# Neighbourhood attention scores in blocks of 32 queries on 64x32 tiles of TensorE

## The chip, the cores and the metric

The kernel runs on one core of a Trainium2 chip. The metric is the device time of one execution in microseconds; the median of three runs before the change is 994.35 us (994.02 to 994.75). The core has five engines with queues of their own: TensorE (PE in the profile; its weight loads are listed apart, as PEld), VectorE (DVE), ScalarE (ACT), GpSimd (POOL) and SyncE (SP), which issues almost all DMAs. Matrix products land in PSUM, which this kernel divides into eight banks of 128 partitions by 512 fp32 values.

## What is computed

One layer over 2048 tokens, laid out as 32 rows by 64 columns, with 16 heads of 64. A query attends to 8 rows by 16 columns around it, with a learned bias for each offset. Cut to what matters:

```python
def neighbourhood_attention(q, k, v, rpb):      # grid of 32 rows x 64 columns
    rs = clip(r - 4, 0, 32 - 8)                  # first key row of query row r
    q_cstart = clip(q_col - 8, 0, 64 - 16)       # first key column of a query column
    s = q . k * 64 ** -0.5 + rpb[head, key_row - r + 7, key_col - q_col + 15]
    s = where(key in the 8 x 16 window, s, -1e30)
    return softmax(s) . v

x = x + (neighbourhood_attention(q, k, v, rpb) * silu(gate)) @ w_out     # q, k, v, gate = rmsnorm(x) @ w_in
out = rmsnorm(x)
```

All matrices are fp32 and the output is compared as fp32.

## The kernel before

**Stages.** Two stages at the start form most of the input projection (groups pp and pv in the profile), then the attention runs, interleaved with the rest of the projection (pp, lines 392 to 396) and later with plain tiles of the output projection (po, lines 1580 to 1584), and a last stage forms the rest of the output projection (py, line 1674). In the profiled execution the attention runs from about 562 to 872 us.

**Cycles.** The attention has 32 cycles. A cycle belongs to a pair of heads p (0 to 7; s in the code is the head within the pair, on partitions 0 to 63 or 64 to 127) and a band T of 8 query rows (0 to 3). `order` (line 1220) runs first all pairs at T=0, then each pair at T=1 and T=2, then all pairs at T=3. A band needs the key rows of `KEY_ROWS`: 11, 15, 15 or 12 rows. The 64 columns are eight strips of 8; the 64 queries of a band and strip g form one block, and its keys lie in the strips g-1 to g+1.

**The order on the engines** is the order in which the program is written; nothing reorders it but semaphores. A cycle m of the main loop (line 1806) issues:

1. `begin(m)`: puts loads for later on a list with due times in units of matmuls (queries, keys, values, bias tables, gate); `due` issues them on SP's queue as the matmuls of `feed` go by.
2. `feed`: matmuls of the projection or of the output. A group of the projection accumulates 24 matmuls in one bank (`group`, line 383); `feed` stops after a given number of them, not at the end of a group. A cycle has some 13.5 of them in the dense part.
3. `normalise(2m-1)`: the second half of the last cycle's probabilities are divided by their sums (POOL, ACT, DVE).
4. `turns(m-1)`: the last cycle's probabilities are transposed on TensorE, 44 transposes of 64 queries by up to 120 keys (line 1357), into six banks (6, 8 and 8 blocks of 64 columns for each half of the partitions). ACT copies three of the banks to SBUF (line 1347), DVE the other three (line 1345).
5. `scores(2m)` and `scores(2m+1)`: each does two of the four `GROUPS` of strips. A group puts two strips on partitions 0 to 63 and 64 to 127 of a bank, so four matmuls of 64 queries (two strips, two heads) run on the four 64x64 quadrants of TensorE (line 1297). The strips 0 and 7 have two strips of keys (`WIDE` 2), the others three. All 64 queries of the band see all key rows of the band: 2 or 3 strips by 8 by 11, 15 or 12 columns. `score_places` (line 1276) gives a bank to each group and head, but puts the first two groups of a head in one bank where 5R fits 512 columns (R is key rows times 8: T=0 and T=3). DVE adds the bias table and finds the extreme (line 1306: the reduction that the page calls CUSTOM_DVE_ANT_0, followed by a read of its accumulator), writing to SBUF and thereby ending the use of the bank; ACT forms the exponential and its sum (line 1312).
6. `values(m-1)`: 16 matmuls of the transposed probabilities with the values into one bank (o, line 1376), on two halves of the columns side by side. DVE multiplies by the gate (line 1380); the result is stored through DRAM (line 1383).

**Buffers.** `banks` has eight buffers; the order of release sets which one is handed out next. `xp` has eight tiles for the scores (line 1303), which are taken anew in each cycle; `mp` has ten tiles for bias tables, of which a cycle at T=0, T=1 or T=3 loads three (`load_bias`, line 1261; T=2 uses those of T=1); `kp` has two tiles for keys (`load_k`, line 1228). In PSUM, a float32 matmul of the program makes two records in the trace; a transpose makes one.

Of the kernel before, what the change touches and what calls it, by code (L numbers as in the profile page):

```python
# [40 lines left out]
BIAS = [(u1 - u0) * 80 for u0, u1 in TYPE_ROWS]  # L41
# [3 lines left out]
def bias_tables(rpb):  # L45
    out = []
    for t, (u0, u1) in enumerate(TYPE_ROWS):
        T = (0, 1, 3)[t]
        got = []
        for G in (1, 0):  # L50
            qr, col, strip, kr, c = np.ogrid[T * 8:T * 8 + 8, :8, :WIDE[G], T * 8 + u0:T * 8 + u1, :8]
            half = []
            for g in GROUPS[G]:
                qc = g * 8 + col
                kc = (FIRST[g] + strip) * 8 + c
# [4 lines left out]
                half.append(np.where(ok, b, np.float32(NEG)).reshape(NP, 2, 64, -1))  # L60
            got.append(np.concatenate(half, axis=2).transpose(0, 2, 1, 3).reshape(NP, 128, -1))
        out += got
    return np.concatenate(out, axis=2)


def linear():
    at, n = {}, 0
    for strips in [(0,), (1, 2), (3, 4), (5, 6), (7,)]:
        for s in range(2):
            for strip in strips:  # L70
                for g in range(max(strip - 1, 0), min(strip + 2, 8)):
                    at[s, strip, g] = n
                    n += 1
    return at
# [3 lines left out]
def build(ctx, tc, x, xr, xt, wg, bias, w_out, n0, nf, out):  # L78
# [540 lines left out]
    def stage_one():  # L619
# [6 lines left out]
        land["x12"] = [rbp([128, 512], F32, "land") for _ in range(2)] + [kp([128, 960], F32, "land")[:, :512] for _ in range(2)]  # L626
# [30 lines left out]
        def value_rows(j):  # L657
            spot = mkp([128, 3, 512], F32, "vs")
            homes = [spot[:, k] for k in range(3)] + [kp([128, 960], F32, "vs")[:, :512]]
# [49 lines left out]
        def step(i):  # L709
# [3 lines left out]
            if i >= 2 * E:  # L713
                seven.after(n, P, then)
            elif P == 1:
                seven.keep(n, kp([128, 960], F32, "p1")[:, :512] if n > 3 else accs[n - 2] if n > 1 else None)
# [205 lines left out]
        def load_u1():  # L922
            for t in range(4):
                U1[t] = accs[t] if t < 2 else ep([128, 512], F32, "u1") if t == 2 else kp([128, 960], F32, "u1")[:, :512]
                nc.sync.dma_start(U1[t], vu1[t])
# [87 lines left out]
    def stage_two():  # L1013
# [11 lines left out]
        def out_rows(k):  # L1025
            def g():
# [5 lines left out]
                homes += [kp([128, 960], F32, "ow")[:, :512] for _ in range(4 - len(homes))]  # L1032
# [61 lines left out]
        def values_product(P, i):  # L1094
# [6 lines left out]
            if P == 1:  # L1101
                U1[i] = ep([128, 512], F32, "u1") if i < 2 else kp([128, 960], F32, "u1")[:, :512]
# [118 lines left out]
    pairs = [(p, T, (h, h + 1)) for p, T in order for h in (0, 2)]  # L1221
    N = len(pairs)
# [5 lines left out]
    def load_k(p, T):  # L1228
# [4 lines left out]
        def keys():  # L1233
            t = kp([128, 960], F32, "kt")
            KT[p, T] = t.rearrange("p (r c) -> p r c", c=GW)
            nc.sync.dma_start(t[:, :n], kd[p][:, r0 * GW:r1 * GW])
# [24 lines left out]
    def load_bias(p, ty):  # L1261
        n = (TYPE_ROWS[ty][1] - TYPE_ROWS[ty][0]) * 8
        a = sum(BIAS[:ty])
        fs = []
        for w in (3 * n, 3 * n, 4 * n):
            t = mp([128, 512], F32, "em")[:, :w]
            EM.setdefault((p, ty), []).append(t)
            fs.append(lambda t=t, a=a, w=w: nc.sync.dma_start(t, bias[p, :, a:a + w]))
            a += w
        i0, i1, e = EM[p, ty]  # L1270
        EM[p, ty] = [[e[:, :2 * n], e[:, 2 * n:]], [i0, i1]]
# [3 lines left out]

    def score_places(cs, R):
        at = {"order": [(C, s) for C in cs for s in range(2)]}
        if cs[0] == 0 and 5 * R <= 512:
            for s in range(2):
                b = bank(5 * R, f"s{s}")  # L1280
                at[0, s], at[1, s] = b[:, :2 * R], b[:, 2 * R:]
        else:
            for C, s in at["order"]:
                at[C, s] = bank(R * WIDE[C], f"s{s}")
        return at

    def scores(i, between=None):
        p, T, cs = pairs[i]
        kt, qt = KT[p, T], QT[p, T]
        r0, r1 = KEY_ROWS[T]  # L1290
        R = (r1 - r0) * 8
        places = score_places(cs, R)
        for C, s in places["order"]:
            for h, g in enumerate(GROUPS[C]):
                c0 = 8 * FIRST[g]
                a = slice(s * 64, s * 64 + 64)
                nc.tensor.matmul(places[C, s][h * 64:h * 64 + 64], qt[a, g * 64:g * 64 + 64],  # L1297
                                 kt[a, :r1 - r0, c0:c0 + 8 * WIDE[C]].rearrange("p r (s c) -> p s r c", c=8),
                                 start=True, stop=True, skip_group_check=True)
        got = [(C, [places[C, s] for s in range(2)]) for C in cs]  # L1300
        ST[i] = st = tiny.tile([128, 12], F32, name="st")
        for j, (C, pst) in enumerate(got):
            X[i, C] = [xp([128, 512], F32, f"x{s}")[:, :R * WIDE[C]] for s in range(2)]
            for s in range(2):
                o = 2 * j + s
                nc.vector.tensor_tensor_reduce(X[i, C][s], pst[s], EM[p, ROW_TYPE[T]][C > 0][s], -1.0, 1e38,  # L1306
                                               OP.add, OP.min, st[:, o:o + 1])
            if between and j == 0:
                between()
            for s in range(2):  # L1310
                o = 2 * j + s
                nc.scalar.activation(X[i, C][s], X[i, C][s], AF.Exp, bias=st[:, o:o + 1], scale=-1.0,  # L1312
                                     accum_out=st[:, 4 + o:5 + o])

    def normalise(i, both=False, between=None):
        st = ST.pop(i)
        nc.vector.reciprocal(st[:, 8:12], st[:, 4:8])  # L1317
        for j, C in enumerate(pairs[i][2]):
            for s in range(2):
                o = 8 + 2 * j + s  # L1320
                if both and j:
                    nc.vector.tensor_scalar(X[i, C][s], X[i, C][s], st[:, o:o + 1], None, op0=OP.mult)
                elif both and s:
                    nc.scalar.activation(X[i, C][s], X[i, C][s], AF.Copy, scale=st[:, o:o + 1])
                else:
                    nc.gpsimd.tensor_scalar(X[i, C][s], X[i, C][s], st[:, o:o + 1], 1.0, op0=OP.mult, op1=OP.mult)  # L1326
        if between:
            between()

    spots = linear()  # L1330

    def turns(m):
# [3 lines left out]
        t = PT[m].rearrange("p (n h c) -> p h n c", h=2, c=64)  # L1336
        ends = (6, 14, 22)
        size = (6, 8, 8)
        ph = {(b, h): bank(size[b] * 64, f"ph{h}") for b in range(3) for h in range(2)}
        left = {(b, h): size[b] for b in range(3) for h in range(2)}  # L1340

        def copy(b, h):
            o, i_ = t[:k, h, ends[b] - size[b]:ends[b]], ph[b, h][:k].rearrange("p (n c) -> p n c", c=64)
            if h:
                nc.vector.tensor_copy(o, i_)  # L1345
            else:
                nc.scalar.activation(o, i_, AF.Copy)  # L1347

        group = {g: C for C in range(4) for g in GROUPS[C]}
        home = lambda n: sum(n // 2 >= e for e in ends)  # L1350
# [545 lines left out]
```

## Time and profile before

| | before |
|---|---|
| median of three runs | 994.35 us (994.02 to 994.75) |
| span of the profiled execution | 993.1 us |
| TensorE busy | 985.0 us, 99% of the span |
| DVE, ACT, POOL busy | 774.3, 542.2, 127.3 us |
| scores on TensorE (line 1297) | 1024 records, 70.8 us busy |
| transposes (line 1357) | 1408 records, 47.0 us busy |
| values (line 1376) | 1024 records, 83.5 us busy |
| bytes moved by DMA | 227.65 MB, mean 229 GB/s |
| granted TensorE clock | 1.00 in all stretches but the last hundred microseconds (0.98) |

The span is measured by the profiler from the first to the last instruction of one execution; the runs are timed apart from it, and their median lies 1.25 us above this span. A row of the groups has the line, the engine, the operation, what it writes and reads, partitions by columns, the count, then the busy time in us and the mean duration in ns of one, then the idle time of the engine before them. Rows of the chain and of a timeline have the start in us, the length in us, and how many instructions are merged in the row; a timeline adds in brackets the idle time before and what ended it. Matmuls overlap, so their durations are longer than their spacing.

### The profile page before, as it was taken

The page shows a single profiled execution, that of the slowest core. Times are in us where ns is not written, and L with a number is a line of the kernel's source. Part 1 is how long each engine was busy: PE and PEld are TensorE (multiplying, and loading weights), DVE is VectorE, ACT ScalarE, POOL GpSimd, SP SyncE. Part 2 cuts the span into 40 slices and gives each one's busy share as a digit, 9 for nine tenths or more (in the row PEclk, how much of TensorE's full clock was granted, in tenths as well). Part 3 has the DMA queues.
Part 4 walks back from the last instruction along what each step waited for, and adds up shares of the span by engine and source line. Part 5 has one row for each costly group of instructions (what it writes and reads, how often), then busy time and mean ns, then how long its engine had stood idle before and what let it go on. Part 6 is the DMA issues. An engine that isn't in the chain of part 4 may idle for free.

```text
span 993.1 us, 19498 instructions
## 1 busy us (share of the span) xinstructions
PE 985.0 (99%) x6892; PEld 789.6 (80%) x6892; DVE 774.3 (78%) x1703; ACT 542.2 (55%) x1310; POOL 127.3 (13%) x204
## 2 busy tenths in 40 slices
PE   9999999999999999999999999999999999999997
PEld 7888888888888888888888777777677777788886
DVE  6899888987565876766775687778889888886866
ACT  7873245455535342343433377778778886663443
POOL 0000001231100000000000022223232321211110
PEclk9999999999999999999999999999999999999999
DMA  8943547777957836557455798978989888996754
GB/s 291 338 128 98 194 135 257 244 240 242 374 157 226 277 117 201 192 174 229 170 179 199 231 290 271 270 237 264 302 247 296 263 249 249 330 382 160 197 153 116
DMA packets 150121, 227.65 MB, mean 229 GB/s; under 512 B 13641, under 2 KB 65097, under 8 KB 150025
## 3 DMA queue, kind: packets, MB, share of 16 engines
q1 hardware_dynamic: 147000, 221.30, 69.5%
q0 software_dynamic: 2592, 4.72, 2.9%
q8 instruction: 54, 0.88, 0.3%
q10 hardware_dynamic: 432, 0.40, 0.1%
q14 instruction: 43, 0.34, 0.1%
HBM read 160.31 MB, written 66.06 MB: 228 GB/s over the span
## 4 chain that ended last, share of the span: by engine, by line
PE 97%; DMA 1%; ACT 1%; DVE 0%; issue 0%; SPq 0%; DVEq 0%
PE pp L448 40%; PE pv L614 13%; PE py L1674 12%; PE o L1376 8%; PE s L1297 6%; PE ph L1357 4%; PE pv L729 2%; PE pp L394 2%; PE pp L392 2%; PE pp L396 2%; PE po L1584 2%; PE po L1582 2%; PE po L1580 2%; DMA kt<-kd 1%; DMA vt<-vd 1%; ACT x L1312 0%
## 5 line engine op out<-in xcount | busy, mean ns | idle before, releaser
L448 PE MATMUL pp<-h,f 128*128 128x512 f32 x576 | 185.5, 390 | 0.0
L448 PE MATMUL pp<-t,f 128*128 128x512 f32 x702 | 171.5, 390 | 0.0
L448 PEld LDWEIGHTS pp<-t,f 128*128 128x128 f32 x702 | 131.7, 188 | 27.6 <-DVE u L461 0.3
L1326 POOL TENSOR_SCALAR x<-x,st 128x360 f32<-128x360 f32 (+5 forms) x160 | 81.5, 524 | 524.0 <-DVE st L1317 524.0
L1312 ACT ACTIVATE x<-x,st 128x360 f32<-128x360 f32 (+5 forms) x256 | 134.1, 525 | 24.7 <-DVE st L1306 24.6
L448 PEld LDWEIGHTS pp<-h,f 128*128 128x128 f32 x576 | 108.1, 188 | 22.7 <-ACT p L456 0.3
L448 PE MATMUL pp<-l,f 128*128 128x512 f32 x288 | 112.2, 389 | 0.0
L1306 DVE CUSTOM_DVE_ANT_0 x<-s,em 128x360 f32<-128x360 f32 (+5 forms) x256 | 102.7, 457 | 3.1 <-issue 1.6
L431 DVE TENSOR_TENSOR f<-raw,f 128x512 fp32r<-128x512 f32 x105 | 75.8, 727 | 19.9 <-ACT f L430 19.8
L1376 PEld LDWEIGHTS o<-pta,vt 120*64 120x64 f32 (+2 forms) x1024 | 68.8, 137 | 22.3 <-DVE st L1306 15.2
L430 ACT ACTIVATE f<-raw 128x512 fp32r<-128x512 f32 x105 | 63.5, 622 | 37.9 <-DVE raw L437 20.1
L1376 PE MATMUL o<-pta,vt 120*64 120x192 f32 (+5 forms) x1024 | 83.5, 316 | 0.0
L1297 PE MATMUL s<-kt,q 64*64 64x360 f32 (+5 forms) x1024 | 70.8, 412 | 0.9 <-DMA kt<-kd 0.9
L1347 ACT ACTIVATE pta<-ph 120x512 f32<-120x512 f32 (+5 forms) x96 | 49.2, 557 | 36.0 <-PE ph L1357 35.9
L1345 DVE COPY pta<-ph 120x512 f32<-120x512 f32 (+5 forms) x96 | 56.1, 638 | 13.3 <-PE ph L1357 13.0
L448 PEld LDWEIGHTS pp<-l,f 128*128 128x128 f32 x288 | 54.1, 188 | 11.3
L1674 PE MATMUL py<-woh,f 128*128 128x512 f32 x192 | 60.8, 390 | 0.0
L614 PE MATMUL pv<-wh,t 128*128 128x512 f32 x176 | 56.2, 389 | 0.0
L448 PE MATMUL pp<-sixths,f 128*128 128x512 f32 x198 | 52.7, 389 | 0.0
L1297 PEld LDWEIGHTS s<-kt,q 64*64 64x64 f32 x1024 | 36.2, 132 | 20.2 <-DVE pta L1345 1.0
L1357 PEld LDWEIGHTS ph<-ident,x 64*120 64x120 f32 (+2 forms) x1408 | 42.5, 128 | 11.3 <-issue 10.9
L430 ACT ACTIVATE f<-s 128x512 fp32r<-128x512 f32 x42 | 26.2, 624 | 45.9 <-DVE s L437 42.6
(227 smaller groups left out, 1875.9 us busy)
## 6 DMA issues: line engine op xcount, KB each, us to landing
raw<-in_wg_dram SPq DMA_DIRECT2D x124, 256.0 KB, 5.2
row<-in_xr_dram SPq DMA_DIRECT2D x32, 256.0 KB, 5.3
vd<-v SPq DMA_DIRECT2D x32, 256.0 KB, 4.9
sgd<-sg SPq DMA_DIRECT2D x32, 256.0 KB, 3.2
q<-qd SPq DMA_DIRECT2D x32, 256.0 KB, 6.8
sgt<-sgd SPq DMA_DIRECT2D x32, 256.0 KB, 7.0
ogd<-og SPq DMA_DIRECT2D x32, 256.0 KB, 3.4
kt<-kd SPq DMA_DIRECT2D x16, 480.0 KB, 6.9
```

The source lines that it names most:

```text
L430: nc.scalar.activation(t[:, 0], src, AF.Copy)
L431: nc.vector.tensor_tensor(t[:, 1], src, t[:, 0].bitcast(F32), OP.subtract)
L448: nc.tensor.matmul(B[n, P], t[:, int(m == 2), c], x[k][int(m == 1)], start=P in (1, 6, 5) and k == 0 and m == 0, stop=k == 3 and m == 2, s ...
L614: nc.tensor.matmul(p, a[:, o], b, start=P in (1, 6, 5) and k == 0 and m == 0, stop=k == 3 and m == 2, skip_group_check=True)
L1297: nc.tensor.matmul(places[C, s][h * 64:h * 64 + 64], qt[a, g * 64:g * 64 + 64], kt[a, :r1 - r0, c0:c0 + 8 * WIDE[C]].rearrange("p r (s c) ...
L1306: nc.vector.tensor_tensor_reduce(X[i, C][s], pst[s], EM[p, ROW_TYPE[T]][C > 0][s], -1.0, 1e38, OP.add, OP.min, st[:, o:o + 1])
L1312: nc.scalar.activation(X[i, C][s], X[i, C][s], AF.Exp, bias=st[:, o:o + 1], scale=-1.0, accum_out=st[:, 4 + o:5 + o])
L1326: nc.gpsimd.tensor_scalar(X[i, C][s], X[i, C][s], st[:, o:o + 1], 1.0, op0=OP.mult, op1=OP.mult)
L1345: nc.vector.tensor_copy(o, i_)
L1357: nc.tensor.transpose(ph[b, h][:k, o:o + 64], X[2 * m + late_, group[g]][s][q, at:at + k], ident[q, q])
L1376: nc.tensor.matmul(o[s * 64:s * 64 + 64, g0 * 64:g1 * 64], vt[:k, strip, s * 64:s * 64 + 64], t[:k, n * 64:(n + g1 - g0) * 64], start=stri ...
L1674: nc.tensor.matmul(B[m, P], t[:, a, c], b, start=P in (1, 6, 5) and k == 0 and i == 0, stop=k == 3 and i == 2, skip_group_check=True)
```

## The change

The 64 queries of a band and strip are split into two halves of 4 rows by 8 columns. A matmul of scores now has 32 queries as its stationary side and runs on a tile of 64x32: two heads by four strips (`quad` 0: strips 0 to 3, 1: strips 4 to 7) fill TensorE's eight such tiles at once. Each half sees its own 11 key rows (8 at the grid's upper and lower edge; `HALF_ROWS`) by 24 columns, for all strips alike. So that strips 0 and 7 can be 24 columns wide too, the tile of keys gets 8 more columns at each end, which hold the neighbouring row's keys or zeros; the bias tables have -1e30 there.

- A cycle's scores are 32 matmuls instead of 16; each half and head has a bank of its own, four for each of the two calls, at every T.
- The tiles of scores are taken once (`make_x`) and hold 3 strips by 120 keys; what a half does not see is set to zero there once (and again by `clear_x` after the last cycle at T=0). Reductions, exponentials and divisions work on three blocks of 88 or 64 columns.
- The transposes are 48 instead of 44, in three rounds of 16, each into two banks of 512 columns that are allocated in that round.
- The values' matmuls read the transposed probabilities in blocks of 32 columns.
- The bias tables come by the kind of half (`top`, `mid`, `end`) and `quad`: four loads for a cycle at T=0 and T=3, two for T=1 and T=2 together. The tiles of `mp` grow from 512 to 528 columns, those of `kp` from 960 to 1024.

The diff, cut to its core:

```diff
-ROW_TYPE = [0, 1, 1, 2]
-TYPE_ROWS = [(0, 11), (-4, 11), (-4, 8)]
-GROUPS = [(0, 7), (2, 1), (4, 3), (6, 5)]
-FIRST = [0, 0, 1, 2, 3, 4, 5, 6]
-WIDE = [2, 3, 3, 3]
+HALF_ROWS = [[(0, 8), (0, 11)], [(0, 11), (4, 11)], [(0, 11), (4, 11)], [(0, 11), (4, 8)]]
+TABLES = {"mid": (8, 4, 11), "top": (0, 0, 8), "end": (28, 24, 8)}
+TABLE_AT = {"mid": 0, "top": 1056, "end": 1824}
...
-    pairs = [(p, T, (h, h + 1)) for p, T in order for h in (0, 2)]
+    pairs = [(p, T, quad) for p, T in order for quad in range(2)]
...
-            t = kp([128, 960], F32, "kt")
-            KT[p, T] = t.rearrange("p (r c) -> p r c", c=GW)
-            nc.sync.dma_start(t[:, :n], kd[p][:, r0 * GW:r1 * GW])
+            KT[p, T] = t = kp([128, 1024], F32, "kt")
+            lo, hi = 8 * (r0 > 0), 8 * (r1 < ROWS)
+            if not lo:
+                nc.gpsimd.memset(t[:, :8], 0.0)
+            if not hi:
+                nc.gpsimd.memset(t[:, 8 + n:16 + n], 0.0)
+            nc.sync.dma_start(t[:, 8 - lo:8 + n + hi], kd[p][:, r0 * GW - lo:r1 * GW + hi])
...
+    kinds_of = lambda T: {0: ("top", "mid"), 3: ("mid", "end")}.get(T, ("mid", "mid"))
+
+    def load_bias(p, T):
         fs = []
+        for kind in dict.fromkeys(kinds_of(T)):
+            w = 48 * TABLES[kind][2]
+            for quad in range(2):
+                t = mp([128, 528], F32, "em")[:, :w]
+                for half in range(2):
+                    if kinds_of(T)[half] == kind:
+                        EM[p, T, quad, half] = [t[:, :w // 2], t[:, w // 2:]]
+                o = TABLE_AT[kind] + quad * w
+                fs.append(lambda t=t, o=o, w=w: nc.sync.dma_start(t, bias[p, :, o:o + w]))
...
+    def keys_of(t, half, T):
+        u, n = HALF_ROWS[T][half]
+        return t.rearrange("p (s k) -> p s k", s=3)[:, :, 8 * u:8 * u + 8 * n]
...
     def scores(i, between=None):
+        p, T, quad = pairs[i]
         kt, qt = KT[p, T], QT[p, T]
+        places = {}
+        for half, (u, n) in enumerate(HALF_ROWS[T]):
+            for s in range(2):
+                places[half, s] = bank(24 * n, f"s{s}")
+            for h in range(4):
+                g = 4 * quad + h
+                for s in range(2):
+                    a = slice(s * 64, s * 64 + 64)
+                    o = u * GW + 8 * g
+                    nc.tensor.matmul(places[half, s][h * 32:h * 32 + 32], qt[a, g * 64 + half * 32:g * 64 + half * 32 + 32],
+                                     kt[a, o:o + n * GW].rearrange("p (r c) -> p r c", c=GW)[:, :, :24]
+                                     .rearrange("p r (s c) -> p s r c", c=8),
+                                     start=True, stop=True, skip_group_check=True)
...
+            xs_ = [keys_of(X[quad, half, s], half, T) for s in range(2)]
+            flat = lambda t: t.rearrange("p (s k) -> p s k", s=3)
             for s in range(2):
+                o = 2 * half + s
+                nc.vector.tensor_tensor_reduce(xs_[s], flat(places[half, s]), flat(EM[p, T, quad, half][s]), -1.0, 1e38,
                                                OP.add, OP.min, st[:, o:o + 1])
...
     def turns(m):
...
+        t = PT[m].rearrange("p (s b n c) -> p b s n c", s=2, b=3, c=64)
+        for b in range(3):
+            ph = [bank(512, f"ph{h}") for h in range(2)]
+            at = (2 - b) * 120
+            for quad in range(2):
+                for half in range(2):
+                    for s in range(2):
+                        for h in range(2):
+                            q = slice(64 * h, 64 * h + 64)
+                            o = s * 256 + half * 128 + quad * 64
+                            nc.tensor.transpose(ph[h][:k, o:o + 64], X[quad, half, s][q, at:at + k], ident[q, q])
+            for h in range(2):
+                o, i_ = t[:k, b, :, h::2], ph[h][:k].rearrange("p (s n c) -> p s n c", s=2, c=64)
+                if h:
+                    nc.vector.tensor_copy(o, i_)
+                else:
+                    nc.scalar.activation(o, i_, AF.Copy)
+        if order[m] == (NP - 1, 0):
+            clear_x()
...
     def values(m):
...
+                b = g0 - strip + 1
+                at = t[:k, (3 * s + b) * 512 + g0 * 32:(3 * s + b) * 512 + g0 * 32 + 32]
+                moving = bass.AP(tensor=at.tensor, offset=at.offset, ap=[at.ap[0], [544, g1 - g0], [256, 2], [1, 32]])
                 nc.tensor.matmul(o[s * 64:s * 64 + 64, g0 * 64:g1 * 64], vt[:k, strip, s * 64:s * 64 + 64],
+                                 moving, start=strip == 0, stop=strip == 7, skip_group_check=True)
```

More of the change, by code (lines that the diff above doesn't have):

```diff
@@ L46, in bias_tables @@
     out = []
[L47 to L55, printed above, removed]
+    for q0, k0, n in TABLES.values():
+        for quad in range(2):
+            got = []
+            for g in range(4 * quad, 4 * quad + 4):
+                qr, col, j, kr, c = np.ogrid[q0:q0 + 4, :8, :3, k0:k0 + n, :8]
+                qc, kc = g * 8 + col, (g - 1 + j) * 8 + c
                 rs = np.clip(qr - KH // 2, 0, ROWS - KH)
@@ L1335, in turns @@
         PT[m] = pt([128, 3072], F32, "pta")
[L1336 to L1350, printed above, removed]
[L1351 to L1362 removed]
+        t = PT[m].rearrange("p (s b n c) -> p b s n c", s=2, b=3, c=64)
+        for b in range(3):
+            ph = [bank(512, f"ph{h}") for h in range(2)]
+            at = (2 - b) * 120
+            for quad in range(2):
+                for half in range(2):
+                    for s in range(2):
+                        for h in range(2):
[10 more added lines that the diff above has]
+            clear_x()
     def values(m):
@@ L1368, in values @@
         vt = VT[p, T]
-        t = PT[m]
-        for C in range(4):
-            X.pop((2 * m + C // 2, C))
+        t = PT.pop(m)
         for strip in range(8):
@@ L1805, in build @@
     attending[0] = True
+    make_x()
     for m in range(cycles + 1):
```

119 lines of the change are left out of this document (36 added, 83 removed).

## Prediction

> **What bounds the kernel now.** I read the page first: busy time by engine, then the chain of work that ended last.
>
> ```profile
> PE 985.0 (99%) x6892; PEld 789.6 (80%) x6892; DVE 774.3 (78%) x1703; ACT 542.2 (55%) x1310; POOL 127.3 (13%) x204
> ...
> PE 97%; DMA 1%; ACT 1%; DVE 0%; issue 0%; SPq 0%; DVEq 0%
> PE pp L448 40%; PE pv L614 13%; PE py L1674 12%; PE o L1376 8%; PE s L1297 6%; PE ph L1357 4%; PE pv L729 2%; PE pp L394 2%; PE pp L392 2%; PE pp L396 2%; PE po L1584 2%; PE po L1582 2%; PE po L1580 2%; DMA kt<-kd 1%; DMA vt<-vd 1%; ACT x L1312 0%
> ...
> L1297 PE MATMUL s<-kt,q 64*64 64x360 f32 (+5 forms) x1024 | 70.8, 412 | 0.9 <-DMA kt<-kd 0.9
> ```
>
> TensorE is busy 99% of the span and is 97% of the chain. What it saves or waits in a cycle of the attention adds to the end one for one; what VectorE (DVE) or ScalarE (ACT) saves counts only where TensorE waits for it. The 512 score matmuls make 1024 records, so each runs in two passes.
>
> Next I read the chain in order of time: a cycle with T=0, one with T=1 or 2 (below "middle"), a disturbed middle one, and three with T=3.
>
> ```profile
> 589.15 0.43 PE pp L396
> ...
> 592.12 0.23 PE pp L396
> 592.34 1.36 PE ph L1357 x44
> 593.70 1.79 PE s L1297 x32
> ...
> 744.45 1.44 PE ph L1357 x44
> 745.89 2.38 PE s L1297 x32
> ...
> 784.67 2.75 PE s L1297 x30
> ...
> 793.38 1.44 PE ph L1357 x44
> ...
> 803.83 1.94 PE s L1297 x32
> ...
> 829.85 1.36 PE ph L1357 x44
> ```
>
> A cycle is transposes (ph), scores (s), values (o), then a stretch of another product (pp or po). In the first two lines this stretch is 13 pieces, about 3 us; a group of that product has 24 matmuls, so it is normally half done when the transposes begin, and **holds a PSUM bank through the attention**.
>
> Per 64x64 quadrant a cycle's scores stream, over both passes, 1936 columns (T=0), 2640 (middle), 2112 (T=3). The lines 1.79, 2.38, 1.94 lie on 0.17 us + 0.838 ns per column: four quadrants side by side.
>
> Then DVE and the weight loads (PEld), as timelines (they start 0.07 earlier than the chain's clock: 744.38 against 744.45):
>
> ```profile
> 592.88 1.75 DVE L1345 COPY pta<-ph 88x384 f32<-88x384 f32 x3 [0.67 <-PE ph L1357]
> ...
> 745.01 1.76 DVE L1345 COPY pta<-ph 120x384 f32<-120x384 f32 x3 [0.59 <-PE ph L1357]
> 746.69 0.40 DVE L1306 CUSTOM_DVE_ANT_0 x<-s,em 128x240 f32<-128x240 f32 x1
> 747.01 0.08 DVE L1306 DVE_READ_ACCUMULATOR2_ANT st<- 128x1 f32 x1
> ...
> 784.48 1.75 DVE L1345 COPY pta<-ph 120x384 f32<-120x384 f32 x3
> 786.46 0.09 DVE L1306 DVE_READ_ACCUMULATOR2_ANT st<- 128x1 f32 x1
> ...
> 794.33 1.75 DVE L1345 COPY pta<-ph 120x384 f32<-120x384 f32 x3
> ...
> 804.93 0.36 DVE L1306 CUSTOM_DVE_ANT_0 x<-s,em 128x192 f32<-128x192 f32 x1 [0.18 <-issue]
> 805.22 0.08 DVE L1306 DVE_READ_ACCUMULATOR2_ANT st<- 128x1 f32 x1
> ...
> 830.78 1.74 DVE L1345 COPY pta<-ph 96x384 f32<-96x384 f32 x3
> ```
>
> ```profile
> 592.27 1.28 PEld L1357 LDWEIGHTS ph<-ident,x 64*88 64x88 f32 x44 [0.35 <-issue]
> ...
> 744.38 1.37 PEld L1357 LDWEIGHTS ph<-ident,x 64*120 64x120 f32 x44 [0.35 <-issue]
> 747.48 0.15 PEld L1297 LDWEIGHTS s<-kt,q 64*64 64x64 f32 x4
> ...
> 783.16 1.37 PEld L1357 LDWEIGHTS ph<-ident,x 64*120 64x120 f32 x44 [0.35 <-issue]
> 786.60 0.14 PEld L1297 LDWEIGHTS s<-kt,q 64*64 64x64 f32 x2
> ```
>
> Here is the cover that decides. Eight banks: one held by the open group, six by the transposes (freed by ACT and DVE copies, L1345/L1347), one free. A middle cycle's scores ask for eight in turn, so **the eighth is the bank of the cycle's first score block**, free only when DVE has done three copies and the first reduction (L1306). In the ordinary cycle that reduction ends at 747.09, and the last loads of the scores come at 747.48. In the disturbed one DVE is late: its first reduction ends at 786.46+0.09=786.55 and the two blocked loads start at 786.60, 0.05 later. Counted from the first transpose they are 3.44 instead of 3.10 us, and the scores last 2.75 instead of 2.38: 0.34 us of lateness cost 0.37, because the second pass, whose weights normally load behind the first, comes another 0.05 late. T=0 and T=3 now put two blocks in one bank (5R is at most 512), ask for six banks, and never meet this wait.
>
> **The change, step by step** (microseconds from a cycle's first transpose, by the weight-load clock).
>
> *Score columns.* Eight tiles of 64x32 instead of four of 64x64. Two passes of a round are 2x264 columns = 0.44, or 2x192 = 0.32. Middle: 2112 columns, not 2640, -0.44. T=0: 1824, not 1936, -0.09. T=3: 1824, not 2112, -0.24. Eight tiles start one after the other: four loads of 0.13 in 0.15 (line 747.48) are 0.006 apart, so +0.025.
>
> *Transposes.* 48 for 44, two side by side. With the scores' 0.17 taken off, a pair is (1.44-0.17)/22 = 0.058 or (1.36-0.17)/22 = 0.054: +0.12 or +0.11. Their first bank is full after 16, not 12: its copy starts as much later.
>
> *Copies and first reduction.* From the groups by shape:
>
> ```profile
> L1345 DVE COPY pta<-ph 120x512 f32<-120x512 f32 x32 | 20.6, 685 | 0.0
> ...
> L1306 DVE CUSTOM_DVE_ANT_0 x<-s,em 128x264 f32<-128x264 f32 x48 | 18.2, 428 | 0.7 <-PE s L1297 0.7
> ...
> L1306 DVE CUSTOM_DVE_ANT_0 x<-s,em 128x240 f32<-128x240 f32 x32 | 11.6, 401 | 0.7 <-issue 0.7
> ...
> L1345 DVE COPY pta<-ph 120x384 f32<-120x384 f32 x16 | 8.9, 557 | 7.1 <-PE ph L1357 6.9
> ```
>
> The first copy grows from 384 to 512 columns: +0.13. The first reduction is 264 wide in the middle (0.40+0.03=0.43 with its read), 192 at T=0 and T=3 (804.93 to 805.30: 0.37). It starts 0.08 before the copies' end (746.69 against 746.77).
>
> *The eighth bank.* The new blocks always take a bank each, so all 31 cycles with transposes and scores ask for eight.
> Middle: the bank is free at 0.63+0.12+1.76+0.13-0.08+0.43+0.05 = 3.04. The fourth round wants it at 1.44+0.12 (scores begin) +0.05+3x0.44 = 2.93. Wait 0.11, plus 0.05 for the second pass.
> T=0 and T=3: free at 0.61+0.11+1.75+0.12-0.08+0.37+0.05 = 2.93; wanted at 1.36+0.11+0.05+0.32+0.44+0.32 = 2.60. Wait 0.33+0.05.
> Behind the blocked load stand, in TensorE's order, all values of the cycle and the rest of the open group; nothing can pass.
>
> *Per cycle.* Middle: +0.12-0.44+0.025+0.16 = -0.14, 16 cycles, -2.2. T=0: +0.11-0.09+0.025+0.38 = +0.42, 7 cycles, +3.0 (the eighth has no transposes before it, about 0). T=3: +0.11-0.24+0.025+0.38 = +0.28, 8 cycles, +2.2. Last transposes +0.1.
>
> *Cycles where DVE is late already.* At 793.38 the copies start at 1.02 instead of 0.75 (0.63+0.12): +0.27; at 829.85, 1.00 instead of 0.72: +0.28. Before, this was free. The disturbed middle cycle paid 0.37 already and would pay 0.57 more than an ordinary one: +0.2. For other such cycles I add 0.25, an estimate. Together +1.0.
>
> *The rest of it, at nothing.* Shorter reductions, exponentials and multiplies lie beside TensorE's work. Whether the forms of three blocks cost more is not in the trace: the copies that write blocks of 64 cost 685 ns for 512, so 0; as a bound I take 0.05 on the first reduction, 31x0.05 = +1.6. The memsets go to GpSimd, 13% busy; keys and zeros are there a cycle ahead. Fixed tiles for the scores' results rotate over the same eight buffers. Values stream the same columns; scores already stream blocks of 8 at full pace, so blocks of 32 cost nothing; a 10% loss on their 2.5 us would be +8 (no row suggests it).
>
> *DMAs.* At T=0 the bias is four loads instead of three, 912 KB instead of 440, at T=3 912 instead of 480, all ahead of the keys on SP's queue.
>
> ```profile
> kt<-kd SPq DMA_DIRECT2D x8, 352.0 KB, 6.7
> ...
> em<-in_bias_dram SPq DMA_DIRECT2D x16, 132.0 KB, 4.7
> ...
> em<-in_bias_dram SPq DMA_DIRECT2D x8, 176.0 KB, 5.3
> ```
>
> ```profile
> 585.29 0.43 SPq L1236 DMA_DIRECT2D kt<-kd  x1
> ```
>
> ```profile
> 575.30:638.10 62.80, 62.80 (x856) 48.83 (x852) 49.34 (x175) 47.02 (x151) 16.17 (x35) 1.00 0.92 281
> ```
>
> The keys asked for at 585.29 land 6.7 later, at 591.99; scores want them at 593.63. 472 KB more at 281 GB/s are 1.7 us and one issue 0.43: 2.1, against a slack of 1.64 and a cycle 0.42 longer. I take 0; the other end is a rival.
>
> **Sum**: -2.2+3.0+2.2+0.1+1.0 = +4.1 on the span of 993.1, and 1.25 lie between this span and the median of 994.35. I take 998.4. A shift of 0.1 in the first reduction's end moves 31 cycles, 3.1 us; so the forecast's own range is 995 to 1001.5.
>
> **Rivals.**
> *The eighth bank is free after all* (the group closed, or the pool hands out another): then columns and transposes alone count: 16x-0.30, 7x+0.05, 8x-0.10, +0.1 = -5.2, **989.1**. For it: TensorE sets the end, and columns fall 20% in the middle. Against: the late loads of the disturbed cycle came 0.05 after a reduction, and the values' loads, which ask for the next bank, have theirs ended by one in 31 cycles of 32:
>
> ```profile
> PEld o L1376 <- DVE st L1306: 15.2, 31, 0.6
> ```
>
> It decides from a first reduction that ends 0.13 us earlier than I have it on average (4.1/31).
> The Trainium skill (TensorE: Matmul & The Clock Gate, "Back-to-back issue gap") gives a floor of about 25 ns between matmul starts; eight starts would then fill 0.20 us where 192 columns ask for 0.16, and this rival would come 2.3 later, at 991.4. The trace shows starts 6 ns apart in bursts of four, and none sustained at 20 ns.
>
> *The eight tiles don't run at once*, only four: every round doubles and the wait for the bank is gone: +1.45 in the middle, +1.55 at T=0, +1.4 at T=3, some 47 in all, **1041**. Against: four quadrants cost no more than their columns. No row has a 32-column tile. The Trainium skill (TensorEngine Tiling (Array Packing), "Available Configurations") lists 64x32 as eight tiles; no run here shows it yet.
>
> *Keys late*: the loads contend, and four of the 15 cycles with T=0 or 3 wait as long as the one wait on record, +3.6 on the forecast, **1002**:
>
> ```profile
> PE s L1297 <- DMA kt<-kd: 0.9, 1, 0.9
> ```
>
> **Chances.** Forecast 0.65, free bank 0.16, keys late 0.14, four tiles 0.05. No change means within 0.2%, 992.4 to 996.3, about what a measurement of this kernel can tell. Of the forecast's 0.65, 0.10 falls there; the free bank is faster, all else slower: faster 0.16, same 0.10, slower 0.74. The range reaches to the free bank at 989.1 and its error, 988, and to late keys, 1002.5; it leaves out the four tiles and tails.
>
> **What would show it.** Right: weight loads of the scores idle before the fourth round, ended by the first reduction (DVE st), most at T=0 and T=3; scores of some 2.1 us in the middle (2.38-0.44+0.025+0.16), 2.1 at T=0 and T=3; transposes 1.47 to 1.56. Wrong: no such idle time and scores of 1.97 and 1.73 (free bank); 3 or more (four tiles); TensorE idle before scores, ended by kt (late keys); values longer than 2.54.

## The result and the profile after

The changed kernel takes 1000.98 us (1000.26 to 1004.66 in four runs), the kernel before, in the same comparison, 994.55 us (994.02 to 995.21). The ratio is 1.0071 with a 95% interval of 1.0052 to 1.0089: slower by 0.7%, where 998.4 us was forecast.

The page of the changed kernel shows more work on TensorE, not less, although the scores' columns fell:

```profile
PE 989.8 (99%) x8044; PEld 795.7 (80%) x8044; DVE 760.5 (76%) x1703; ACT 532.5 (53%) x1310; POOL 123.7 (12%) x228
...
L1296 PE MATMUL s<-kt,q 64*32 64x264 f32 (+1 forms) x2048 | 68.6, 375 | 1.4 <-issue 1.3
```

TensorE's busy time grew by 4.8 us, on the same 99%. To see where, take two rows of the chain in both kernels: the last long stretch of the projection, which ends where the attention begins, and the last product, which begins where it ends. The kernel before:

```profile
389.04 171.36 PE pp L448 x756
...
872.54 114.48 PE py L1674 x504
```

The changed kernel:

```profile
390.79 172.62 PE pp L430 x756
...
878.41 115.22 PE py L1666 x504
```

| us | before | after | difference |
|---|---|---|---|
| ahead of the attention (389.04 + 171.36; 390.79 + 172.62) | 560.40 | 563.41 | +3.01 |
| attention, to the start of py | 312.14 | 315.00 | +2.86 |
| last product | 114.48 | 115.22 | +0.74 |
| span | 993.1 | 999.8 | +6.7 |

**More than half of the loss lies outside the attention**, in matmuls that the diff does not touch: the same 756 matmuls take 171.36/756 = 226.7 ns each before and 228.3 ns after. The tables of the experiments below are made in the same way. (The expectations count the same stretches a little differently: 560.7 us ahead of the attention for the kernel before where these rows give 560.40, and an attention of 313 to 314 us for the changed kernel where they give 315.00.)

Inside the attention the cycles are where the prediction looked. The chain of the changed kernel shows a cycle with T=0, the late keys (they were there before too), a middle cycle, one with T=3, and the last transposes:

```profile
605.46 1.47 PE ph L1346 x48
606.93 2.06 PE s L1296 x64
...
720.77 1.28 issue
...
748.55 1.55 PE ph L1346 x47
750.10 2.10 PE s L1296 x64
...
824.75 1.48 PE ph L1346 x48
826.22 2.01 PE s L1296 x64
...
873.43 0.63 PE ph L1346 x16
874.05 0.90 ACT pta L1352 x2
875.01 0.60 ACT pta L1352
875.66 2.75 PE o L1368 x32
```

Per cycle, transposes and scores together: T=0 1.47+2.06 against 1.36+1.79, +0.38; middle 1.55+2.10 against 1.44+2.38, -0.17; T=3 1.48+2.01 against 1.36+1.94, +0.19. Times 7, 16 and 8: +2.7, -2.7, +1.5. The row at 720.77 is the late keys: they are asked for at 712.53 and land 9.4 us later, at 721.93, and the scores begin at 722.05. The other piece is the end: the last cycle's values wait for copies by ScalarE (ACT) that nothing covers.

The wait itself can be read from the weight loads (PEld) and DVE, here for the same T=0 cycle, in timelines of short windows. A row that merges several loads shows the first one's start:

```profile
605.38 1.39 PEld L1346 LDWEIGHTS ph<-ident,x 64*88 64x88 f32 x48 [0.35 <-issue]
606.86 1.00 PEld L1296 LDWEIGHTS s<-kt,q 64*32 64x32 f32 x48
608.04 0.13 PEld L1296 LDWEIGHTS s<-kt,q 64*32 64x32 f32 x2 [0.18 <-DVE pta L1350]
...
608.31 0.18 PEld L1296 LDWEIGHTS s<-kt,q 64*32 64x32 f32 x14
```

```profile
606.10 1.88 DVE L1350 COPY pta<-ph 88x512 f32<-88x512 f32 x3 [1.46 <-PE ph L1346]
607.91 0.34 DVE L1306 CUSTOM_DVE_ANT_0 x<-s,em 128x192 f32<-128x192 f32 x1
```

Three rounds of scores load without a pause (48 loads in 1.00 us). The fourth round wants two banks. The first of them, the seventh bank of the cycle, is the one that DVE copies last: the copies end at 606.10+1.88 = 607.98, its load comes at 608.04. The other is the eighth: the first reduction ends at 607.91+0.34 = 608.25, and the next loads come at 608.31, 0.06 later. That is 608.31-605.38 = 2.93 us after the first transpose. A middle cycle and one with T=3:

```profile
748.48 1.49 PEld L1346 LDWEIGHTS ph<-ident,x 64*120 64x120 f32 x48 [0.36 <-issue]
...
751.52 0.18 PEld L1296 LDWEIGHTS s<-kt,q 64*32 64x32 f32 x14
```

```profile
824.68 1.40 PEld L1346 LDWEIGHTS ph<-ident,x 64*96 64x96 f32 x48 [0.35 <-issue]
...
827.68 0.18 PEld L1296 LDWEIGHTS s<-kt,q 64*32 64x32 f32 x14 [0.18 <-DVE st L1306]
```

They come 3.04 and 3.00 us after the first transpose. The first reductions of these two cycles:

```profile
751.04 0.42 DVE L1306 CUSTOM_DVE_ANT_0 x<-s,em 128x264 f32<-128x264 f32 x1
...
827.20 0.42 DVE L1306 CUSTOM_DVE_ANT_0 x<-s,em 128x264 f32<-128x264 f32 x1
```

They end at 751.46 and 827.62, and the loads follow 0.06 later each time. The view of waits gives more to the copies than to the reductions (at 608.31 it names no releaser at all), though the reduction came last in each of these three cycles:

```profile
PEld s L1296 <- DVE pta L1350: 3.8, 18, 0.4
...
PEld s L1296 <- DVE st L1306: 1.3, 7, 0.2
```

### The profile page after: what moved, and what is told of

Read it like the earlier page. It is cut to its first block, busy times and chain, and to the rows that moved or that the text cites. A ratio compares the mean times of both kernels' runs of the same rounds, so it can differ in the third digit from the quotient of the medians.

```text
span 999.8 us, 21845 instructions
## 1 busy us (share of the span) xinstructions
PE 989.8 (99%) x8044; PEld 795.7 (80%) x8044; DVE 760.5 (76%) x1703; ACT 532.5 (53%) x1310; POOL 123.7 (12%) x228
## 4 chain that ended last, share of the span: by engine, by line
PE 99%; DMA 0%; ACT 0%; issue 0%; DVE 0%; ACTq 0%
PE pp L430 40%; PE pv L596 13%; PE py L1666 12%; PE o L1368 8%; PE s L1296 7%; PE ph L1346 5%; PE pp L376 2%; PE pp L374 2%; PE pv L711 2%; PE pp L378 2%; PE po L1576 2%; PE po L1574 2%; PE po L1572 2%; DMA raw<-in_wg_dram 0%; ACT pta L1352 0%
## 5 line engine op out<-in xcount | busy, mean ns | idle before, releaser
L1312 ACT ACTIVATE x<-x,st 128x264 f32<-128x264 f32 (+1 forms) x256 | 124.4, 487 | 25.2 <-DVE st L1306 25.2
L1328 POOL TENSOR_SCALAR x<-x,st 128x264 f32<-128x264 f32 (+1 forms) x160 | 74.7, 483 | 249.6 <-DVE st L1317 235.8
L1306 DVE CUSTOM_DVE_ANT_0 x<-s,em 128x264 f32<-128x264 f32 (+1 forms) x256 | 90.3, 407 | 1.7 <-issue 1.2
L1350 DVE COPY pta<-ph 120x512 f32<-120x512 f32 (+2 forms) x96 | 60.3, 682 | 22.9 <-PE ph L1346 22.9
L1352 ACT ACTIVATE pta<-ph 120x512 f32<-120x512 f32 (+2 forms) x96 | 50.2, 594 | 46.0 <-PE ph L1346 46.0
L1296 PE MATMUL s<-kt,q 64*32 64x264 f32 (+1 forms) x2048 | 68.6, 375 | 1.4 <-issue 1.3
L1346 PEld LDWEIGHTS ph<-ident,x 64*120 64x120 f32 (+2 forms) x1536 | 46.1, 128 | 11.3 <-issue 10.9
L1296 PEld LDWEIGHTS s<-kt,q 64*32 64x32 f32 x2048 | 38.8, 105 | 18.9 <-DVE pta L1350 3.8
```

Of the source, the lines that this page charges most:

```text
L1296: nc.tensor.matmul(places[half, s][h * 32:h * 32 + 32], qt[a, g * 64 + half * 32:g * 64 + half * 32 + 32], kt[a, o:o + n * GW].rearrange(" ...
L1306: nc.vector.tensor_tensor_reduce(xs_[s], flat(places[half, s]), flat(EM[p, T, quad, half][s]), -1.0, 1e38, OP.add, OP.min, st[:, o:o + 1])
L1312: nc.scalar.activation(xs_[s], xs_[s], AF.Exp, bias=st[:, o:o + 1], scale=-1.0, accum_out=st[:, 4 + o:5 + o])
L1328: nc.gpsimd.tensor_scalar(t, t, st[:, o:o + 1], 1.0, op0=OP.mult, op1=OP.mult)
L1346: nc.tensor.transpose(ph[h][:k, o:o + 64], X[quad, half, s][q, at:at + k], ident[q, q])
```

## The experiments

Two theories stood against each other for the 3.75 us outside the attention. The first: the wider tiles of `mp` and `kp` move the places in SBUF that the same pools hold earlier and later, as operands of the large products. The second: the change's other setup or its loads. For the attention the theory was the wait for the seventh and eighth bank, with late keys as rival.

**e1_pad.** The kernel before, with nothing but the tile sizes of the changed one:

```diff
-            t = mp([128, 512], F32, "em")[:, :w]
+            t = mp([128, 528], F32, "em")[:, :w]
...
-            t = kp([128, 960], F32, "kt")
+            t = kp([128, 1024], F32, "kt")
```

> The kernel before, with nothing of the change but its two wider tiles: bias tiles of 528 columns (2112 bytes apart instead of 2048) and key tiles of 1024; computation and instructions are the kernel's before. Theory (where the tiles lie sets the pace of the products that read them): the same 2459 matmuls ahead of the attention take 563.2 to 563.7 us instead of 560.7, the product after the attention some 0.7 us more, and the time is 3.0 to 3.8 us above the kernel before. Rival (the changed kernel's matmuls outside the attention are slower by its executions' chance, or by its larger traffic): no more than 0.5 us above the kernel before.

Measured: 997.51 us against 994.85, ratio 1.0027 (1.0017 to 1.0038). Its chain:

```profile
390.24 172.62 PE pp L448 x756
...
874.07 115.10 PE py L1674 x504
```

+2.46 ahead of the attention, +0.62 in the last product, with the old scores untouched (311.21 in the attention). The long stretch takes 172.62, the same as in the changed kernel. So most of the loss outside the attention is the tile sizes. The whole kernel loses 2.7 us, a little less than the 3.0 to 3.8 that were expected.

**e2_kp.** The kernel before with `kp` alone at 1024 columns.

> The kernel before with the wider key tiles alone (1024 columns); bias tiles stay 512 wide, so that all tiles behind the keys move by 512 bytes and none changes its distance. If the odd distance of the bias tiles is what costs, this is within 0.4 us of the kernel before; if any move of the tiles does, or the wider key tiles, it is 1 us or more above it.

Measured: 994.72 us, ratio 0.9995 (0.9983 to 1.0007), no loss; the long stretch takes 171.36 and the last product 114.48, as in the kernel before. This moves every tile of `mp` by 512 bytes and keeps their distance at 2048. It is the tiles of 528 columns, 2112 bytes apart, that cost.

**e8_shift64 and e9_shift128.** Is it the odd distance, or where a tile starts? The kernel before with a gap ahead of `mp`, all tiles still 2048 bytes apart:

```diff
+    gap = ctx.enter_context(tc.tile_pool(name="gap", bufs=1)).tile([128, 16], F32, name="gap")
...
+    nc.vector.memset(gap, 0.0)
```

> The kernel before with a gap of 64 bytes ahead of the pool of middle tiles: each tile starts 64 bytes later, the distance from one to the next stays 2048 bytes. If it is the start of a tile that counts (not a multiple of 256 bytes any more, and so for all of them), the matmuls that read them space above 226.6 ns, the work ahead of the attention takes 2 us or more longer than 560.7, and the time is 996.5 or more. If only an odd distance between tiles counts, it stays within 0.4 us of the kernel before, 994.2 to 995.2.

Measured: 999.05 us, ratio 1.0046 (1.0034 to 1.0058). With 32 columns in the gap:

> The kernel before with a gap of 128 instead of 64 bytes ahead of the pool of middle tiles, which keep their distance of 2048 bytes. If a start at a multiple of 128 bytes is enough, the time is that of the kernel before, 994.2 to 995.2, and the work ahead of the attention takes 560.4 to 561 us. If it takes 256 bytes, it loses as the gap of 64 bytes did: 563 us or more ahead of the attention, 997 to 999.5 in all.

Measured: 998.87 us, ratio 1.0039 (1.0023 to 1.0054). The chain of the gap of 64 bytes, then that of 128:

```profile
391.51 172.50 PE pp L450 x756
...
875.23 115.44 PE py L1676 x504
```

```profile
390.90 172.68 PE pp L450 x756
...
875.96 115.16 PE py L1676 x504
```

+3.61 and +3.18 ahead of the attention, +0.96 and +0.68 behind it. An odd distance is not needed for the loss; the start counts. Every start of a tile of `mp` in the kernel before, and in e2_kp, is a multiple of 256 bytes; a gap of 64 or 128 bytes costs at least as much as the odd distance did. One thing these runs do not separate: the gap also moves the pools that lie behind `mp` (`ep`, `lp`, `ev`, `rbp`, `tiny`) by 64 or 128 bytes, and the ten tiles of 528 columns, 64 bytes longer each, move them by 640, which is 128 off a multiple of 256 as well. No run moved `mp` alone or those pools alone.

**e6_em512.** The cure, in the changed kernel: the bias lies in DRAM by quad and head, so that one tile holds both halves of one head (192+264 = 456 columns, as many loads per cycle at T=0 and T=3, four smaller ones at T=1) and 512 columns suffice.

```diff
-            for quad in range(2):
-                t = mp([128, 528], F32, "em")[:, :w]
...
+        for quad in range(2):
+            for s in range(2):
+                t = mp([128, 512], F32, "em")[:, :w]
```

> The changed kernel with the bias laid out by head, so that its tiles are 512 columns as before (2048 bytes from one to the next); the scores, waits and copies are those of the changed kernel. If the odd distance of the tiles is what the work outside the attention loses, the work ahead of the attention comes back to 560.5 to 561.0 us and the last product to 114.1 to 114.3, the attention stays at 313 to 314, and the time is 997 to 998.5. Rival: that loss belongs to something else of the change (its loads of the bias, its constants), then 1000.5 to 1002.

Measured: 998.20 us, ratio to before 1.0035 (1.0023 to 1.0047).

```profile
388.47 171.36 PE pp L432 x756
...
874.95 114.48 PE py L1668 x504
```

Both stretches are back to the very figures of the kernel before, 171.36 and 114.48, and with them all of the loss outside the attention: the work ahead ends at 559.83, 0.57 earlier than in the kernel before, so single profiles differ by that much there. The attention, 315.12, is that of the changed kernel. The medians put the gain at 1000.98-998.20 = 2.8 us.

**e3_one_bank.** The changed kernel; at T=0 and T=3 the two halves of a head share a bank (192+264 columns fit), so a cycle's scores ask for four banks there, not eight (the expectation below says six, which is the count of the kernel before).

```diff
-                places[half, s] = bank(24 * n, f"s{s}")
+                if T in (0, 3):
+                    if half == 0:
+                        both = bank(24 * (n + HALF_ROWS[T][1][1]), f"s{s}")
+                        places[0, s], places[1, s] = both[:, :24 * n], both[:, 24 * n:]
+                else:
+                    places[half, s] = bank(24 * n, f"s{s}")
```

> The changed kernel, with the two halves of a head in one bank where they fit (T=0 and T=3: 192+264 columns of 512), so that these cycles ask for six banks instead of eight again. Theory (the fourth round waits for the bank of the first reduction): scores at T=0 and T=3 fall from 2.06 and 2.01 us to 1.73, the middle cycles stay at 2.10, and the time falls by 0.33x7+0.28x8 = 4.5 us against the changed kernel. Rival (eight 64x32 tiles stream more slowly than their columns, or weight loads bound them): scores stay at 2.0 or more, and the time within 0.7 us.

Measured: 996.99 us, ratio to before 1.0019 (1.0008 to 1.0030), 4.0 less than the changed kernel. Its chain has, for T=0, the middle and T=3:

```profile
605.63 1.70 PE s L1301 x64
...
746.63 2.10 PE s L1301 x64
...
822.51 1.70 PE s L1301 x64
```

The scores fall by 0.36 and 0.31 where the wait was taken away and stay at 2.10 where it was left. 15 cycles at these prices are 5.0; the attention is 309.84, 5.2 less.

The same rows decide a point left open before. A T=0 cycle streams 1824 columns; 0.17+0.838x1.824 = 1.70. Eight tiles of 64x32 run at once and the rounds of 192 columns cost their columns; within a set of eight the matmuls of this cycle start 6 to 7 ns apart. The Trainium skill (TensorEngine Tiling (Array Packing), "Available Configurations") has 64x32 as eight tiles; the trace agrees. The Trainium skill's floor of about 25 ns between starts (TensorE: Matmul & The Clock Gate, "Back-to-back issue gap") would make two rounds of 192 columns, 16 starts each, 0.40 instead of 0.32 and this cycle 1.86; the measured 1.70 decides against it here.

**e4_act_copy.** The changed kernel; ACT instead of DVE makes the sixth copy, so that the first reduction need not stand behind three copies.

```diff
-                if h:
+                if h and b < 2:
```

> The changed kernel, with one of VectorE's three copies of the transposes given to ScalarE (the last one), so that the first reduction ends some 0.6 us earlier. Theory: the wait of the middle cycles is gone, scores there 1.97 instead of 2.10; at T=0 and T=3 the bank of the fourth ScalarE copy is wanted in its place, free at about 2.79 against a want of 2.60, and scores fall from 2.06 and 2.01 to some 1.9; together 0.13x16+0.13x15 = 4 us against the changed kernel. Rival (the tiles themselves are slow): scores unchanged, and the time within 0.7 us.

Measured: 996.80 us, ratio 1.0021 (1.0012 to 1.0030), 4.2 less than the changed kernel. Chain of a middle cycle and of one with T=3, then a wait:

```profile
749.43 1.98 PE s L1296 x64
...
824.10 1.84 PE s L1296 x64
```

```profile
PE s L1296 <- DMA kt<-kd: 2.3, 2, 1.7
```

Scores fall by 0.12 to 1.98 in the middle. At T=0 and T=3 they fall to 1.92 and 1.84, by 0.14 and 0.17, about half of the wait there: in the T=3 cycle the last round now waits until ACT's four copies end at 825.29 and loads at 825.34. The gain is partly eaten in the profiled run by keys that come late at T=0.

**e5_both.** The two edits together.

> The changed kernel with both waits taken away at once: the two halves of a head share a bank in the first and the last strip, and ScalarE takes the last copy of the values' operand. If the two waits are separate prices, scores take about 1.7 us in the first and last strip and 1.96 in the middle, the attention is 5.5 to 6.5 us shorter than in the changed kernel, and the time is about 994.5 (994 to 996); the work ahead of and behind the attention keeps its +2.7 and +0.7 us. Rival: both edits buy the same slack, so together they give no more than one alone, 996 to 997.5.

Measured: 994.13 us, ratio 1.0000 (0.9989 to 1.0011).

```profile
390.41 172.62 PE pp L430 x756
...
605.46 1.70 PE s L1301 x64
...
744.79 1.98 PE s L1301 x64
...
820.18 1.70 PE s L1301 x64
...
870.84 115.22 PE py L1671 x504
```

All scores run near their columns' pace (2112 columns in the middle are 0.17+1.77 = 1.94), and the attention, 870.84-563.03 = 307.81, is 7.2 shorter than in the changed kernel, more than expected, and 4.3 shorter than before. The wait of the middle cycles and that of the first and last band are separate prices; the two edits overlap a little (4.0 and 4.2 us alone, 6.85 together, by the medians), since each alone shortens the scores at T=0 and T=3. What the columns gain, the places of the tiles and the last cycle take: no change in all.

**e7_all.** e5 with e6's tiles, and in the last cycle the transposes ahead of the last matmuls of the feed, which then run while the last copies are made:

```diff
+        if m == cycles:
+            turns(m - 1)
         feed(a * 0.4, 8 if a > 12 else 4)
-        if m:
+        if m and m < cycles:
             turns(m - 1)
```

> The tiles of 512 columns, one bank for both halves of a head in the first and last strip, the last copy on ScalarE, and in the last cycle the transposes ahead of the last few matmuls of the feed, which then run while the last copies are made. If the four prices add up, 1001 - 3 - 6 - 0.9 = about 991 (989.5 to 992.5), which is 0.2 to 0.5% faster than the kernel before. Rival: with the waits gone the cycles run ahead of the keys and values that the feed makes, transposes wait for keys at the first strips (about 1 to 2.5 us at one or two of the cycles), and the time is 993 to 995, no faster than before.

Measured: 992.33 us (989.23 to 995.23), ratio 0.9973 (0.9960 to 0.9986): faster than the kernel before, though at the upper end of what was expected. The rows behind:

```profile
712.62 1.60 PE ph L1353 x47
714.22 1.94 issue
716.16 3.70 PE s L1303 x64
...
865.04 1.48 PE ph L1353 x48
...
867.64 2.54 PE o L1375 x32
```

The last cycle no longer waits for its copies (values 1.1 us behind the transposes, with matmuls of the feed between). But at 714.22 TensorE waits 1.94 us and the scores behind take 3.70 instead of 1.98. This cycle's keys are asked for at 707.54, 6.7 us before TensorE is there, and the loads of keys around it (690 to 735 us) land 6.3 to 8.1 us after they are asked for. The trace has no landing for this one and names no releaser for the wait, so here the keys are inferred; e10 tries it. Of the rival in this expectation the mechanism came, at a lower price.

**e10_keys.** e7, with the keys asked for earlier in the cycle:

```diff
-            later_loads([load_q(*nx), load_k(*nx)], 7, 5)
+            later_loads([load_k(*nx), load_q(*nx)], 2, 5)
```

> The kernel with all four mends, and in each cycle the next cycle's keys are asked for 10 matmuls of the feed earlier, ahead of its queries and bias (2 and 7 instead of 12 and 7 after the cycle begins). If what is left of lost time in the attention, and the scatter of the runs from 989 to 995, is keys that come late, TensorE no longer waits at the scores' start for 2 us, the attention is 305 to 306.5 us, and the median 989.5 to 991 with less scatter. Rival: the loads only change places and what follows (bias, gate, values) is late in their stead: 991.5 to 994.

Measured: 990.82 us (990.29 to 993.49), ratio 0.9968 (0.9955 to 0.9980), the lowest median here: 0.32% below the kernel before. The interval overlaps that of e7, so a gain over e7 is not shown. The wait in the middle cycle is gone, and the middle cycles are alike within 0.1 us; but the profiled run (992.96 us) waits elsewhere, and its attention is 310.45 us, not the 305 to 306.5 that were expected:

```profile
PE s L1303 <- DMA q<-qd: 3.3, 2, 2.3
```

The queries of two T=0 cycles now come late in the keys' stead. Both cases came, in part: the median is better than the rival's range and worse than most of the first, and what the loads of the T=0 cycles still cost from run to run stays open.

## Why the prediction was right, and where it was not

**The eighth bank: right, in mechanism and in size.** Worked out were 3.04 us from first transpose to the blocked loads in the middle, measured 3.04; 2.93 at T=0, measured 2.93; 2.93 at T=3, measured 3.00. The T=3 figure took a first reduction of 192 columns, but there the first half has 11 rows: the row in the changed kernel is 0.42 long for 264. For the same reason the fourth round is wanted later, and the wait came out smaller: 2.01-1.70 = 0.31 instead of 0.38. In the middle it was 2.10-1.98 = 0.12 instead of 0.16, at T=0 2.06-1.70 = 0.36 instead of 0.38. What the prediction did not name is that the seventh bank is late too, by the last copy; that wait is shorter and ends before the eighth's, and in the middle cycles e4 shows that both go with one copy moved.

**Columns and transposes: right.** Transposes are 1.47 to 1.55. Without the waits scores take 1.70, 1.98 and 1.70, where 1.73, 1.97 and 1.73 were named as the mark of a free bank.

**Per cycle: right in sign, and near in size.** Middle -0.17 for -0.14, T=0 +0.38 for +0.42, T=3 +0.19 for +0.28; together +1.5 where +3.0 was summed (-2.2+3.0+2.2).

**Cycles where DVE is late: mis-sized, +1.0.** In the changed kernel the scores of the seven T=0 cycles take 2.06 each and those of T=3 from 1.94 to 2.15 around 2.01; there is no group of late cycles at +0.25. The disturbed middle cycle takes 2.56, 0.46 over its neighbours where 0.57 was said and 0.37 was paid before. With one T=3 cycle at +0.14 and one middle cycle at +0.09 that is some 0.3 together.

**Last transposes: mis-sized, +0.1.** The step counted their number and left out the copies behind them, which in the last cycle no scores cover. From first transpose to values it is 875.66-873.43 = 2.23 us, where the kernel before took 1.36. Chain of the kernel before, then DVE's copies there:

```profile
868.56 1.36 PE ph L1357 x44
869.92 2.61 PE o L1376 x32
```

```profile
869.21 1.74 DVE L1345 COPY pta<-ph 96x384 f32<-96x384 f32 x3
```

There the values begin at 869.92, while DVE copies until 870.95: the code before fills the banks strip by strip, so that the first values need the first copies only. In the changed kernel each round of transposes holds one of the three neighbouring strips for all blocks, so that the first values need copies of the last round; they begin 0.05 after ACT's last copy ends at 875.61. The values themselves are 0.14 longer. That is +1.0, and e7 shows it can be covered.

**"The rest of it, at nothing": wrong, and the largest error.** That step priced tiles, memsets and copies within the attention and found cover for each. It never asked what else lives in `mp`: before and after the attention the pool's slots hold operands of the large products, and making its tiles 528 columns wide moved most of them, and the pools behind, off their 256-byte starts. Measured: +3.01 ahead and +0.74 behind, where the step had nothing; e1 shows 2.46 and 0.62 of it with the tile sizes alone, and e6 shows all of it gone with 512 columns.

The total was near because these errors partly cancel: 1.5 too much in the cycles, 0.7 too much for late DVE, against 0.9 too little at the end and 3.75 outside. That 1000.98 still lies below the upper end of 1001.5 is luck: the range was argued from the end of the first reduction, and what used it up was work that no term of the sum held. Within the attention's +2.86, 1.5 lie in the cycles and 1.0 at the end; the one wait for keys, 0.9 before and 1.28 after, adds some 0.4.

**The rivals.** Four tiles only fell: the scores follow their columns. Late keys cost 0.4 and not 3.6, since only one cycle waits and it waited before; with the other waits gone, late loads show again in e7 and e10. The free bank, -5.2, is what e5 shows when the waits are removed: -4.3 in the attention with the last cycle's +1.0 in it, so -5.3. That sum was sound; it needed the banks that the change had taken.

## What to carry to other kernels

When a change widens a tile, find every other use of its pool and of the pools behind it: a larger slot moves operands of work that the diff doesn't touch, and padding it may cost more than the tile gains. When work becomes shorter on the engine that sets the end, count the buffers it asks for per cycle against those that are free, by the time each comes free; giving two results one bank was worth 4 us here, more than the change itself lost in the cycles. And look at the last round of a loop by itself: what covers a copy in all other rounds may be missing there.

## What the hardware showed that was not expected

The products of 128x128 by 128x512 run slower when the tile that streams through TensorE starts off a multiple of 256 bytes in SBUF. In the kernel before, matmuls of the first products start 226.5 to 226.9 ns apart for every slot of `mp` that they stream. In the changed kernel the slots lie 2112 bytes apart, so only the slots 0, 4 and 8 start at a multiple of 256 bytes. Matmuls that stream the others start, on average over 21 or 42 of them, 230 to 237 ns apart; slots 0 and 4 show 226.8 and 226.6. Slot 8 shows 239.8 in spite of its start, but its matmuls alternate with those of slot 9, which is off, while slots 0 and 4 alternate with each other or with tiles that start right. So the interval grows when either of two neighbouring matmuls streams a tile that is off.

That is not all of it. Of the 3.0 us ahead of the attention, 1.5 fall on the 250 matmuls that stream a tile off 256 bytes and 0.3 on the 48 just ahead of such a one; the rest lies on other matmuls, whose tiles start at a multiple of 256. With the gap of 64 bytes those of the unmoved pools `qp` and `vp` start 231.6 and 229.3 ns apart instead of 226.7. Whether TensorE's own reads are slow, or other engines and transfers that use moved tiles disturb it, no run here separates. The Trainium skill (SBUF — State Buffer, "Operand start alignment") asks only for a multiple of the element size and says that its runs timed nothing; the price here is some 3 to 4.6 us in 675 for starts 64, 128 or 192 bytes off.
